# A two-layer streaming encoder on one core: norm scales moved from the weights to the activations, and the second sigmoid of stick-breaking left in its PSUM bank

## Chip, cores and metric

The kernel runs on one core of a Trainium2 chip, in one launch. The metric is the device time in microseconds (us) from start to end; less is better. TensorE multiplies, VectorE, ScalarE and GpSimd do the work around it, and all DMAs of the kernel are issued from SyncE's queue. The profile calls them PE (PEld is its weight load), DVE, ACT, POOL and SP.

## What is computed

Two layers over 2048 prompt tokens and 64 sample tokens, 1024 wide, all in float32. Every layer is one mixer:

```python
xn = rms(x, norm_g)
aq, ak, av, ag, bcq, bckv, bkr, bg, cq, ck, cv, cg, mq, mg = split_in(xn @ w_in)
...                                    # four head groups A, B, C, M of 4 heads each
y = rms(heads(y, 16), out_g) * silu(gates)
x = x + y @ w_out
```

Group A is band attention, B latent attention, M attention into 256 memory tokens. Group C is stick-breaking, without a softmax:

```python
z = einsum('bqhd,bkhd->bhqk', q, k) * Dh ** -0.5
log_1m = where(mask, log_sigmoid(-z), 0.0)
tail = cumsum(log_1m, reverse=True) - log_1m
w = where(mask, exp(log_sigmoid(z) + tail), 0.0)
```

So a weight is sigmoid(z) of its key times the product of sigmoid(-z) over all later keys.

## The kernel before

Rows of 128 tokens are tiles: 16 prompt tiles and one for the sample, in three blocks of 6, 6 and 5. Two generators make the program together. One runs the projections (`p_stream`): for each block, layer and chunk of 256 output columns, 8 steps over the 1024 inputs. The other runs attention (`attention`): units of two query tiles and four key tiles, group after group; a unit's scores, transposes and products with V are three stages that run on different units at the same time. A rule of target positions interleaves both, and the framework's scheduler then orders each engine's queue, which runs in that order.

Float32 products are made from two roundings, high and low: x = xh + xl and w = wh + wl, and a step is three matmuls (L402, L403, L405: xh wh, xh wl, xl wh; for narrow chunks the first two are one, L400).

`weights` (L297) makes both parts of a chunk. It loads blocks of two steps (`raw`, 128 x 2 x 256). For each step GpSimd multiplies by the norm's gain `gc`, a column with one value per input row, and rounds (L304); VectorE makes the low part from the same product (L305). The tiles `wh` are 8, as many as one chunk has steps, so the next chunk's first write waits until the last row tile of this chunk has used the buffer.

`prep` (L239) makes the parts of the activations. For each half of a row tile TensorE transposes four blocks into one bank (`ptx`, L259), ScalarE copies 512 columns to `xh` with rounding (L266), VectorE subtracts into `xl` (`sub_r`, L136). A sample tile is folded: its low part takes the free half of the 128 columns.

`Stick` (L1070) is group C. `step` makes the scores of one query tile against up to four key tiles in a bank `ps` (L855, L856; the pool `ps_st` has 5 banks, for transposes and `prep` too), adds a mask on the diagonal (L1090), and ScalarE writes sigmoid(-z) to `cc` and sigmoid(z) to `s`, both in SBUF (L1093, L1094). After that unit's round of other units' transposes and products, `s1b` copies the carry (L1109), scans on VectorE (L1110) with min(state x cc, cc), from the last key to the first, and multiplies on GpSimd (L1113). Then `s2` transposes `s` (L900), ScalarE casts to `ph` (L903), VectorE makes the low part (L136), and TensorE multiplies with V (L925). `cc` shares its buffers (tag `kr`) with a key tile of group B.

Of the kernel before, what the change touches and what calls it, by code (L numbers as in the profile page):

```python
# [7 lines left out]
F32 = mybir.dt.float32  # L8
# [56 lines left out]
def hybrid_step(  # L65
# [51 lines left out]

    mhalf = const.tile([128, 32], F32, name="mhalf")
    V.memset(mhalf, -0.5)

    NQ = 3
    qbuf = [const.tile([128, 2, 256], F32R, name=f"qbuf{i}") for i in range(NQ)]
# [113 lines left out]
        if left[tag] == 0:  # L236
            done.add(tag)

    def prep(load, norm, acts, t, split):  # L239

        xs = []
        for q in range(2):
            xs.append(pj.tile([128, 512], F32, tag="xin", name="xin", bufs=2))
            load(xs[q], q)
        yield 0
        xh = pj.tile([128, 8, 128], F32R, tag="xh", name="xh", bufs=MAXB)
        xl = pj.tile([128, 8, 128], F32R, tag="xl", name="xl", bufs=MAXB)
        st = None
        if norm:
            st = pj.tile([128, 4], F32, tag="xst", name="xst", bufs=MAXB + 1)  # L250
        acts[t] = (xh, xl, st)
        for q in range(2):
            x = xs[q]
            if norm:
                A.activation(out=xl[:, q * 4:q * 4 + 4].rearrange("p a b -> p (a b)"), in_=x, func=ACTF.Square,
                             accum_out=st[:, q:q + 1])
            pt = ps_st.tile([128, 4, 128], F32, name="ptx")
            for k in range(4):
                T.transpose(pt[:, k, :], x[:, k * 128:(k + 1) * 128], ident)  # L259
            ks = slice(q * 4, q * 4 + 4)  # L260
            if t == SAMP and split:
                A.copy(out=xl[:, ks], in_=pt)
                copy_r(xh[:, ks, 0:64], xl[:, ks, 0:64].bitcast(F32))
                sub_r(xh[:, ks, 64:128], pt[:, :, 64:128], xl[:, ks, 64:128])
            else:
                A.copy(out=xh[:, ks], in_=pt)  # L266
                sub_r(xl[:, ks], pt, xh[:, ks])
            yield 1024
        if norm:
            V.tensor_tensor(out=st[:, 2:3], in0=st[:, 0:1], in1=st[:, 1:2], op=ALU.add)  # L270
            V.tensor_scalar(out=st[:, 2:3], in0=st[:, 2:3], scalar1=1.0 / 1024, scalar2=EPS,
                            op0=ALU.mult, op1=ALU.add)
            rpow(st[:, 3:4], st[:, 2:3], 1)
# [22 lines left out]

    def weights(job, c0, w, out):  # L297

        gc = job.gcols()

        def split(raw, k):
            hl = pj.tile([128, 512], F32R, tag="wh", name="wh", bufs=8)
            h, lo = hl[:, 0:w], hl[:, w:2 * w]
            G.tensor_scalar(out=h, in0=raw, scalar1=gc[:, k:k + 1], scalar2=1.0, op0=ALU.mult, op1=ALU.mult)  # L304
            V.scalar_tensor_tensor(out=lo, in0=raw, scalar=gc[:, k:k + 1],  # L305
                                   in1=h.bitcast(F32), op0=ALU.mult, op1=ALU.subtract)
            out.append((hl[:, 0:2 * w], h, lo))

        n = 2
        src = job.wsrc[:, 8 * c0:8 * (c0 + w)].rearrange("p (k c) -> p k c", k=8)  # L310
        raws = []
        for k in range(0, 8, n):
# [2 lines left out]
            raws.append(raw)  # L315
            yield 0
            if k > 0:
                for i in range(n):
                    split(raws[-2][:, i, 0:w], k - n + i)
                    yield 0  # L320
        for i in range(n):
            if i:
                yield 0
            split(raws[-1][:, i, 0:w], 8 - n + i)

    def p_stream(jobs):
        chunks = [(j,) + c for j in jobs for c in j.chunks]
# [32 lines left out]
        def start_prep(j, t):  # L360

            if (j, t) not in ready:
                ready.add((j, t))
                begin(j)
                preps[j, t] = prep(j.loader(t), j.norm, j.acts, t, j.folds(t))
                next(preps[j, t])

        def prep_tile(j, t):
# [700 lines left out]

    class Stick(Unit):  # L1070
        def s1a(self):
            self.sb, self.cc, self.k = [], [], 0

        def more(self):
            return self.k < self.n
# [1 line left out]
        def step(self):  # L1077
# [11 lines left out]
            if mask is not None:  # L1089
                V.tensor_tensor(out=ps[:, w - 128:w], in0=ps[:, w - 128:w], in1=mask, op=ALU.add)  # L1090
            s = s_tile()
            cc = at.tile([128, 512], F32, tag="kr", name="cc", bufs=4)
            A.activation(out=cc[:, 0:w], in_=ps[:, 0:w], func=ACTF.Sigmoid, scale=-0.125)  # L1093
            A.activation(out=s[:, 0:w], in_=ps[:, 0:w], func=ACTF.Sigmoid, scale=0.125)  # L1094
            self.sb.append(s)
            self.cc.append(cc)
            self.k += 1

        def s1b(self):
            p = self.pair  # L1100
            carry = p.setdefault("carry", [None, None])
            for i, (a, e) in enumerate(self.ranges):
                w = (e - a) * 128
                s, cc = self.sb[i], self.cc[i]
                r = at.tile([128, 513], F32, tag="r", name="r", bufs=3)
                if carry[i] is None:
                    G.memset(r[:, w:w + 1], 1.0)
                else:
                    V.tensor_copy(r[:, w:w + 1], carry[i][:, 0:1])  # L1109
                V.tensor_tensor_scan(r[:, 0:w][:, ::-1], cc[:, 0:w][:, ::-1], cc[:, 0:w][:, ::-1], r[:, w:w + 1],  # L1110
                                     ALU.mult, ALU.min)
                carry[i] = r
                G.tensor_tensor(out=s[:, 0:w], in0=s[:, 0:w], in1=r[:, 1:w + 1], op=ALU.mult)  # L1113

    def load_kv(d, g, h, c, n, sample):
        kv = at.tile([128, 2, 512], F32R, tag="kv", name="kv", bufs=5)
# [454 lines left out]
```

## Time and profile before

| | |
|---|---|
| median of 3 runs | 3382.83 us (3377.99 to 3388.35) |
| profiled execution, time | 3392.03 us |
| profiled execution, span | 3390.2 us |
| TensorE busy | 3177.9 us (94%), 24486 matmuls |
| VectorE busy | 2728.9 us (80%) |
| ScalarE busy | 1939.0 us (57%) |
| GpSimd busy | 1598.4 us (47%) |
| granted TensorE clock, mean | 0.985 |

Busy shares are means over stages with different limits, and matmuls overlap each other, so a busy TensorE isn't one at its peak; the number of matmuls in a stretch tells more.

### The profile page before, as it was taken

What the parts mean: (1) busy time and instruction counts of PE and PEld (TensorE: products, weight loads), DVE (VectorE), ACT (ScalarE), POOL (GpSimd) and SP (SyncE); (2) the same over time, 40 slices, a digit from 0 to 9 for tenths busy, and PEclk for the clock granted to TensorE, in tenths of its full rate; (3) what the DMA queues carried; (4) which work ended last, traced back from release to release, by engine and by line L of the source; (5) the groups of instructions that cost most, each with busy time, mean ns of one, the idle gap of its engine ahead of it and who ended that gap; (6) DMA issues with size and microseconds to landing.
All of it is one profiled execution on the core that took longest, in us unless ns stands there. A gap on an engine that the chain in (4) does not pass through costs nothing. (4 is left out here: it accounts for less than half of the span.)

```text
span 3390.2 us, 75857 instructions
## 1 busy us (share of the span) xinstructions
PE 3177.9 (94%) x24486; PEld 3029.8 (89%) x24486; DVE 2728.9 (80%) x7976; ACT 1939.0 (57%) x5336; POOL 1598.4 (47%) x2353
## 2 busy tenths in 40 slices
PE   8999899899999998999999899988999999999898
PEld 7899899789999988999999788978898998888898
DVE  5686777999788789887778977899878888776994
ACT  4455655567665555566556665656646566654651
POOL 4564455666344256542434635477424454112563
PEclk9999999999999998999999999999999999999999
DMA  6555776435656656565566567634455766556534
GB/s 198 168 147 165 205 203 191 131 101 155 172 155 192 194 165 166 141 191 154 145 186 193 146 177 209 194 111 118 140 142 160 207 193 192 151 149 179 153 110 147
DMA packets 576123, 558.95 MB, mean 165 GB/s; under 512 B 70960, under 2 KB 478000, under 8 KB 575728
## 3 DMA queue, kind: packets, MB, share of 16 engines
q1 hardware_dynamic: 575728, 554.10, 58.3%
q8 instruction: 196, 3.21, 0.4%
q14 instruction: 199, 1.63, 0.2%
HBM read 378.21 MB, written 173.75 MB: 163 GB/s over the span
## 5 line engine op out<-in xcount | busy, mean ns | idle before, releaser
L403 PE MATMUL pp<-wh,xh 128*128 128x256 f32 x4416 | 1268.4, 291 | 33.6 <-DVE wh L305 32.3
L402 PE MATMUL pp<-wh,xh 128*128 128x256 f32 x4416 | 1259.8, 290 | 21.9 <-ACT ev L437 14.4
L405 PE MATMUL pp<-wh,xl 128*128 128x256 f32 (+1 forms) x4416 | 1250.5, 285 | 0.6 <-DVE xl L136 0.4
L403 PEld LDWEIGHTS pp<-wh,xh 128*128 128x128 f32 x4416 | 839.9, 191 | 64.0 <-DVE wh L305 51.3
L402 PEld LDWEIGHTS pp<-wh,xh 128*128 128x128 f32 x4416 | 837.5, 191 | 39.2 <-ACT ev L437 18.5
L405 PEld LDWEIGHTS pp<-wh,xl 128*128 128x128 f32 x4416 | 845.1, 192 | 9.3 <-DVE xl L136 0.8
L304 POOL TENSOR_SCALAR wh<-raw,gc 128x256 fp32r<-128x256 f32 (+1 forms) x848 | 500.1, 604 | 301.6 <-PE pp L405 146.3
L925 PE MATMUL ot<-ph,kv 128*128 128x256 f32 (+1 forms) x3104 | 591.8, 294 | 34.3 <-DVE ph L136 18.8
L903 ACT CAST ph<-pt 128x512 fp32r<-128x512 f32 (+2 forms) x840 | 451.0, 551 | 259.6 <-PE pt L900 231.0
L136 DVE TENSOR_TENSOR ph<-pt,ph 128x512 fp32r<-128x512 f32 (+2 forms) x840 | 525.9, 634 | 68.7 <-ACT ph L903 64.8
L900 PE MATMUL pt<-identr,s 128*128 128x128 f32 x3056 | 509.7, 277 | 25.2 <-POOL s L1113 8.0
L925 PEld LDWEIGHTS ot<-ph,kv 128*128 128x128 f32 x3104 | 458.7, 191 | 56.5 <-DVE ph L136 28.0
L1113 POOL TENSOR_TENSOR s<-s,r 128x512 f32<-128x512 f32 (+3 forms) x328 | 359.6, 1102 | 311.4 <-DVE r L1110 136.9
L305 DVE SCALAR_TENSOR_TENSOR wh<-raw,gc,wh 128x256 fp32r<-128x256 f32 (+1 forms) x848 | 472.5, 582 | 25.0 <-POOL wh L304 22.9
L1110 DVE TENSOR_TENSOR_SCAN r<-cc,r 128x512 f32<-128x512 f32 (+3 forms) x328 | 406.5, 1250 | 15.9 <-ACT cc L1093 14.4
L139 POOL TENSOR_TENSOR st<-st,mhalf 128x4 f32<-128x4 f32 (+1 forms) x312 | 283.3, 913 | 270.9 <-DVE st L463 240.4
L855 PE MATMUL ps<-kv,qbuf 128*128 128x512 f32 (+3 forms) x1024 | 376.7, 371 | 25.7 <-DVE ph L136 5.4
L900 PEld LDWEIGHTS pt<-identr,s 128*128 128x128 f32 x3056 | 361.8, 141 | 43.6 <-POOL s L1113 12.4
L856 PE MATMUL ps<-kv,qbuf 128*128 128x512 f32 (+3 forms) x1024 | 351.1, 345 | 0.0
L437 ACT ACTIVATE ev<-pp,xst 128x256 f32<-128x256 f32 (+1 forms) x424 | 199.9, 473 | 161.7 <-PE pp L405 118.4
L1093 ACT ACTIVATE cc<-ps 128x512 f32<-128x512 f32 (+3 forms) x328 | 178.2, 544 | 192.5 <-DVE ps L1090 153.7
L1051 ACT ACTIVATE s<-s,nm 128x512 f32<-128x512 f32 (+3 forms) x328 | 212.6, 651 | 107.2 <-DVE nm L1043 74.3
(171 smaller groups left out, 5128.9 us busy)
## 6 DMA issues: line engine op xcount, KB each, us to landing
raw<-in_w_in SPq DMA_DIRECT2D x288, 256.0 KB, 3.5
kv<-kvC SPq DMA_DIRECT2D x128, 256.0 KB, 4.3
kv<-kvB SPq DMA_DIRECT2D x128, 256.0 KB, 4.4
kv<-kvA SPq DMA_DIRECT2D x96, 256.0 KB, 4.5
raw<-in_w_out SPq DMA_DIRECT2D x96, 256.0 KB, 3.4
y<-y SPq DMA_DIRECT2D x136, 128.0 KB, 2.5
xin<-y SPq DMA_DIRECT2D x64, 256.0 KB, 3.5
qC<-kt SPq DMA_DIRECT2D x34, 256.0 KB, 3.0
```

The costliest lines, as they stand in the source:

```text
L136: (eng or V).tensor_tensor(out=dst, in0=src, in1=hi.bitcast(F32), op=ALU.subtract)
L304: G.tensor_scalar(out=h, in0=raw, scalar1=gc[:, k:k + 1], scalar2=1.0, op0=ALU.mult, op1=ALU.mult)
L305: V.scalar_tensor_tensor(out=lo, in0=raw, scalar=gc[:, k:k + 1], in1=h.bitcast(F32), op0=ALU.mult, op1=ALU.subtract)
L402: T.matmul(pp, lhsT=xh[:, k], rhs=wh, start=(k == 0), stop=False)
L403: T.matmul(pp, lhsT=xh[:, k], rhs=wl, start=False, stop=end)
L405: T.matmul(pp[:, 0:w], lhsT=xl[:, k], rhs=wh, start=False, stop=(k == 7))
L855: T.matmul(ps[:, 0:w], lhsT=q[:, 0, qs], rhs=kt[:, c0:c0 + w], start=True, stop=False)
L900: T.transpose(pt[:, (u + x) * 128:(u + x + 1) * 128], self.p_of(i, j), ident)
L903: A.copy(out=ph[:, 0:w], in_=pt[:, 0:w])
L925: T.matmul(ot[:, e * lo, il[0]:il[0] + n], lhsT=p["vt"](j), rhs=phl[:, e, u * 128:(u + n) * 128], start=start and e == 0, stop=stop and e ...
L1110: V.tensor_tensor_scan(r[:, 0:w][:, ::-1], cc[:, 0:w][:, ::-1], cc[:, 0:w][:, ::-1], r[:, w:w + 1], ALU.mult, ALU.min)
L1113: G.tensor_tensor(out=s[:, 0:w], in0=s[:, 0:w], in1=r[:, 1:w + 1], op=ALU.mult)
```

## The change

Two edits in one.

Norm scales: the gain is no longer multiplied into the weights but into the transposed activations. In `prep` ScalarE makes four scaled copies, one per block of 128 inputs with its column of `gc`, and VectorE makes the low part with the same column, also in four. `weights` is left with splitting: ScalarE copies two steps at once with rounding, GpSimd subtracts. VectorE has no part in it. The tiles `wh` hold two steps each, and are 4.

Stick-breaking: sigmoid(z) is made first, then sigmoid(-z) overwrites the scores in their bank, and the scan reads it there. Its second input is a column of ones, broadcast: min(state x cc, 1). Carry, scan and product move from `s1b` to the end of `step`.

```diff
+    one = const.tile([128, 1], F32, name="one")
+    V.memset(one, 1.0)
...
-    def prep(load, norm, acts, t, split):
+    def prep(load, norm, acts, t, split, gc):
...
-            if t == SAMP and split:
-                A.copy(out=xl[:, ks], in_=pt)
+            fold = t == SAMP and split
+            hi, cs = (xl, slice(64, 128)) if fold else (xh, slice(0, 128))
+            lo = xh if fold else xl
+
+            for k in range(4):
+                kk = q * 4 + k
+                A.activation(out=hi[:, kk], in_=pt[:, k], func=ACTF.Copy, scale=gc[:, kk:kk + 1])
+            for k in range(4):
+                kk = q * 4 + k
+                V.scalar_tensor_tensor(out=lo[:, kk, cs], in0=pt[:, k, cs], scalar=gc[:, kk:kk + 1],
+                                       in1=hi[:, kk, cs].bitcast(F32), op0=ALU.mult, op1=ALU.subtract)
+            if fold:
                 copy_r(xh[:, ks, 0:64], xl[:, ks, 0:64].bitcast(F32))
-                sub_r(xh[:, ks, 64:128], pt[:, :, 64:128], xl[:, ks, 64:128])
-            else:
-                A.copy(out=xh[:, ks], in_=pt)
-                sub_r(xl[:, ks], pt, xh[:, ks])
...
-        gc = job.gcols()
-
-        def split(raw, k):
-            hl = pj.tile([128, 512], F32R, tag="wh", name="wh", bufs=8)
-            h, lo = hl[:, 0:w], hl[:, w:2 * w]
-            G.tensor_scalar(out=h, in0=raw, scalar1=gc[:, k:k + 1], scalar2=1.0, op0=ALU.mult, op1=ALU.mult)
-            V.scalar_tensor_tensor(out=lo, in0=raw, scalar=gc[:, k:k + 1],
-                                   in1=h.bitcast(F32), op0=ALU.mult, op1=ALU.subtract)
-            out.append((hl[:, 0:2 * w], h, lo))
-
         n = 2
+
+        def split(raw):
+            hl = pj.tile([128, n, 512], F32R, tag="wh", name="wh", bufs=4)
+            h, lo = hl[:, :, 0:w], hl[:, :, w:2 * w]
+            A.copy(out=h, in_=raw)
+            G.tensor_tensor(out=lo, in0=raw, in1=h.bitcast(F32), op=ALU.subtract)
+            for i in range(n):
+                out.append((hl[:, i, 0:2 * w], h[:, i], lo[:, i]))
+
...
-            cc = at.tile([128, 512], F32, tag="kr", name="cc", bufs=4)
-            A.activation(out=cc[:, 0:w], in_=ps[:, 0:w], func=ACTF.Sigmoid, scale=-0.125)
             A.activation(out=s[:, 0:w], in_=ps[:, 0:w], func=ACTF.Sigmoid, scale=0.125)
+
+            cc = ps[:, 0:w]
+            A.activation(out=cc, in_=cc, func=ACTF.Sigmoid, scale=-0.125)
+            carry = p.setdefault("carry", [None, None])
+            r = at.tile([128, 513], F32, tag="r", name="r", bufs=3)
+            if carry[i] is None:
+                G.memset(r[:, w:w + 1], 1.0)
+            else:
+                V.tensor_copy(r[:, w:w + 1], carry[i][:, 0:1])
+            V.tensor_tensor_scan(r[:, 0:w][:, ::-1], cc[:, ::-1], one.to_broadcast([128, w]), r[:, w:w + 1], ALU.mult, ALU.min)
+            carry[i] = r
+            G.tensor_tensor(out=s[:, 0:w], in0=s[:, 0:w], in1=r[:, 1:w + 1], op=ALU.mult)
             self.sb.append(s)
-            self.cc.append(cc)
             self.k += 1
 
         def s1b(self):
-            p = self.pair
...
+            pass
```

The scheduler orders the queues anew. On VectorE, at the diagonal unit of tiles 10 and 11 of one head in layer 0 (the rows named `r<-cc,r` are the scan, `wh<-raw,gc,wh` the weights' low part), it stood like this before:

```order
L1090 TENSOR_TENSOR ps<-ps,tri 128x128
L947 TENSOR_TENSOR opark<-ob,opark 128x2x64
L1110 SCALAR_TENSOR_TENSOR r<-cc,r 128x384
L305 SCALAR_TENSOR_TENSOR wh<-raw,gc,wh 128x256 x2
L1110 SCALAR_TENSOR_TENSOR r<-cc,r 128x512
L305 SCALAR_TENSOR_TENSOR wh<-raw,gc,wh 128x256
L1109 COPY r<-r 128x1
```

and in the changed kernel, at the same unit of one head:

```order
L1093 TENSOR_TENSOR ps<-ps,tri 128x128
L1105 SCALAR_TENSOR_TENSOR r<-ps,r,one 128x384
L1104 COPY r<-r 128x1
L1105 SCALAR_TENSOR_TENSOR r<-ps,r,one 128x512
L1104 COPY r<-r 128x1
L138 TENSOR_TENSOR ph<-pt,ph 128x512 x2
```

The weight split is gone from between the scans, and the scan reads the bank `ps`.

On ScalarE, where the last of the three units of tiles 10 and 11 begins in one head (`ph<-pt` is the cast of transposed weights, `ev<-pp` the eviction of a projection), the order before was:

```order
L903 CAST ph<-pt 128x512
L931 COPY os<-ot 128x256
L497 CAST kt<-ptk 128x256
L903 CAST ph<-pt 128x384
L1093 ACTIVATE cc<-ps 128x512
L1094 ACTIVATE s<-ps 128x512
L437 ACTIVATE ev<-pp,xst 128x256
L1093 ACTIVATE cc<-ps 128x512
```

and in the changed kernel:

```order
L906 CAST ph<-pt 128x512
L934 COPY os<-ot 128x256
L500 CAST kt<-ptk 128x256
L906 CAST ph<-pt 128x384
L312 CAST wh<-raw 128x2x256 x3
L440 ACTIVATE ev<-pp,xst 128x256
L1095 ACTIVATE s<-ps 128x512
L1098 ACTIVATE ps<-ps 128x512
```

Three weight copies now stand ahead of the eviction and the sigmoids, and the sigmoids have changed places.

## Rows read from the trace of the kernel before

**Rows 1.** The page: busy us, share of the span and instructions of each engine.
```profile
span 3390.2 us, 75857 instructions
...
PE 3177.9 (94%) x24486; PEld 3029.8 (89%) x24486; DVE 2728.9 (80%) x7976; ACT 1939.0 (57%) x5336; POOL 1598.4 (47%) x2353
```

**Rows 2.** Busy us (instructions) by stretch: five with stick-breaking, then one without.
```profile
core 0: us, PE busy (x) PEld busy (x) DVE busy (x) ACT busy (x) POOL busy (x), PEclk, DMA share, GB/s
600.00:800.00 200.00, 180.28 (x1376) 168.42 (x1375) 188.08 (x363) 129.42 (x310) 136.47 (x164) 1.00 0.42 115
1200.00:1500.00 300.00, 279.01 (x2088) 262.69 (x2086) 265.50 (x595) 170.86 (x422) 163.43 (x214) 0.97 0.58 162
1800.00:1900.00 100.00, 94.74 (x762) 91.92 (x761) 88.25 (x262) 63.89 (x201) 56.44 (x81) 0.98 0.59 170
2200.00:2400.00 200.00, 176.50 (x1304) 163.15 (x1302) 190.13 (x351) 125.29 (x296) 143.07 (x160) 0.98 0.39 109
3100.00:3300.00 200.00, 183.79 (x1388) 172.66 (x1387) 189.93 (x352) 119.36 (x265) 116.05 (x137) 0.98 0.51 141
sum 1000.00, PE 914.31 PEld 858.84 DVE 921.88 ACT 608.81 POOL 615.45; mean PE 182.86 PEld 171.77 DVE 184.38 ACT 121.76 POOL 123.09
...
800.00:1200.00 400.00, 391.36 (x3095) 378.02 (x3095) 320.65 (x1056) 234.89 (x654) 166.13 (x267) 1.00 0.64 180
```

**Rows 3.** The same five stretches, instructions of L305, L1110 and L266 alone, sums.
```profile
sum 1000.00, DVE 135.31; mean DVE 27.06
...
sum 1000.00, DVE 352.92; mean DVE 70.58
...
sum 1000.00, ACT 26.32; mean ACT 5.26
```

**Rows 4.** Groups, busy us and mean ns: split by line, scan, product by form.
```profile
L304 POOL TENSOR_SCALAR wh<-raw,gc 128x256 fp32r<-128x256 f32 (+1 forms) x848 | 500.1, 604 | 301.6 <-PE pp L405 146.3
...
L305 DVE SCALAR_TENSOR_TENSOR wh<-raw,gc,wh 128x256 fp32r<-128x256 f32 (+1 forms) x848 | 472.5, 582 | 25.0 <-POOL wh L304 22.9
...
L1110 DVE TENSOR_TENSOR_SCAN r<-cc,r 128x512 f32<-128x512 f32 x224 | 327.1, 1470 | 6.8 <-ACT cc L1093 6.4 <-issue 0.2
L1113 POOL TENSOR_TENSOR s<-s,r 128x512 f32<-128x512 f32 x224 | 279.4, 1253 | 189.3 <-DVE r L1110 68.2 <-ACT s L1094 27.0 <-ACT ph L903 12.6
```

**Rows 5.** Groups by form: what stands nearest to the new copies and scalings.
```profile
L136 DVE TENSOR_TENSOR xl<-ptx,xh 128x512 fp32r<-128x512 f32 x136 | 92.2, 682 | 16.7 <-ACT xh L266 16.3
...
L266 ACT CAST xh<-ptx 128x512 fp32r<-128x512 f32 x136 | 79.4, 595 | 33.0 <-PE ptx L259 32.2
...
L501 DVE SCALAR_TENSOR_TENSOR kt<-ptk,qg,kt 128x256 fp32r<-128x256 f32 x102 | 48.3, 473 | 3.7 <-ACT kt L500 3.6
L255 ACT ACTIVATE xl<-xin 128x512 fp32r<-128x512 f32 x76 | 48.0, 635 | 51.7 <-DMA xin<-in_x_prompt 24.6 <-DMA xin<-x 21.0 <-DMA xin<-in_x_sample 3.7
...
L1066 DVE SCALAR_TENSOR_TENSOR opark<-opark,f,ob 128x64 f32<-128x64 f32 x192 | 45.1, 274 | 14.7 <-PE ob L941 14.4
...
L437 ACT ACTIVATE ev<-pp,xst 128x160 f32<-128x160 f32 x32 | 12.7, 396 | 3.7 <-PE pp L405 2.9 <-PE ot L925 0.6
```

**Rows 6.** VectorE: a scan in the timeline; additions 256 wide, groups by form.
```profile
651.64 1.27 DVE L1110 TENSOR_TENSOR_SCAN r<-cc,r 128x512 f32<-128x512 f32 x1
...
L474 DVE TENSOR_TENSOR nrm<-ev,st 128x256 f32<-128x256 f32 x106 | 58.2, 549 | 17.2 <-POOL st L139 10.0 <-DMA o_akp<-nrm 4.8 <-PE ptk L494 1.4
...
L838 DVE TENSOR_TENSOR xr<-pp,xr 128x256 f32<-128x256 f32 x128 | 52.7, 414 | 33.4 <-PE pp L405 17.9 <-DMA xr<-x 13.8 <-DMA xr<-in_x_prompt 1.2
```

**Rows 7.** Waits: total us, times, longest; GpSimd, then TensorE.
```profile
POOL wh L304 <- PE pp L405: 146.3, 39, 28.5
...
POOL wh L304 <- PE pp L403: 88.1, 25, 18.2
...
PE pp L403 <- DVE wh L305: 32.3, 49, 2.1
...
PE pp L402 <- ACT ev L437: 14.4, 13, 4.1
```

More of the change, by code (lines that the diff above doesn't have):

```diff
@@ L317, in weights @@
             if k > 0:
[L318 to L322, printed above, removed]
+                split(raws[-2][:, :, 0:w])
                 yield 0
-            split(raws[-1][:, i, 0:w], 8 - n + i)
+        split(raws[-1][:, :, 0:w])
     def p_stream(jobs):
@@ L364, in start_prep @@
                 begin(j)
-                preps[j, t] = prep(j.loader(t), j.norm, j.acts, t, j.folds(t))
+                preps[j, t] = prep(j.loader(t), j.norm, j.acts, t, j.folds(t), j.gcols())
                 next(preps[j, t])
@@ L1071, in s1a @@
         def s1a(self):
-            self.sb, self.cc, self.k = [], [], 0
+            self.sb, self.k = [], 0
         def more(self):
@@ L1091, in step @@
             s = s_tile()
-            cc = at.tile([128, 512], F32, tag="kr", name="cc", bufs=4)
-            A.activation(out=cc[:, 0:w], in_=ps[:, 0:w], func=ACTF.Sigmoid, scale=-0.125)
             A.activation(out=s[:, 0:w], in_=ps[:, 0:w], func=ACTF.Sigmoid, scale=0.125)
+            cc = ps[:, 0:w]
[9 more added lines that the diff above has]
+            G.tensor_tensor(out=s[:, 0:w], in0=s[:, 0:w], in1=r[:, 1:w + 1], op=ALU.mult)
             self.sb.append(s)
-            self.cc.append(cc)
             self.k += 1
         def s1b(self):
-            p = self.pair
[L1101 to L1113, printed above, removed]
+            pass
     def load_kv(d, g, h, c, n, sample):
```

## The prediction, made before the changed kernel was run

> **What bounds the kernel now.** I read the page's busy times first. TensorE is busy for 3177.9 of 3390.2 us and VectorE for 2728.9, while ScalarE has 1939.0 and GpSimd 1598.4 [rows 1]. Averages hide stages, so I then read busy time by stretch. Five stretches hold most of the scans of stick-breaking (group C). In these 1000 us VectorE is busy for 921.9 and TensorE for only 914.3, with 6918 matmuls (the five counts added). In 800 to 1200 us, which holds almost no scan, TensorE is busy for 391.4 of 400 us and does 3095 matmuls, 7.74 per us against 6.92 [rows 2]. So there are two regimes: outside the scans TensorE sets the pace; inside them VectorE is nearly full and TensorE goes without work for 86 us and runs slower. What fills VectorE there: the scans take 352.9 us and the weight split (L305) 135.3 us [rows 3]. The waits agree: the largest wait of TensorE shown is for the low half of a weight from VectorE, 32.3 us [rows 7].
>
> **Part 1, the weights.** VectorE loses all 848 operations of L305, 472.5 us, of which 135.3 us lie in the five stretches [rows 3, 4]. GpSimd loses 848 scalings (500.1 us) and gets 424 subtractions of two blocks at once. The nearest row is the product of stick-breaking, also two inputs, 512 wide: 1.253 us [rows 4]. 424 x 1.253 = 531 us, at most 31 us more; I count nothing, since GpSimd has the most slack. ScalarE gets 424 copies. The nearest row is its pass over 512 elements in SBUF, 0.635 us [rows 5]: 424 x 0.635 = 269 us. Some 29% of the split lies in the five stretches (135.3 of 472.5), so at most 122 copies, 77 us.
>
> **Part 2, the norm scales in `prep`.** 136 half tiles take one copy (0.595 us) and one subtraction (0.682 us) [rows 5]. Each becomes four scaled copies 128 wide on ScalarE, with a column as scale, and four combined operations on VectorE. The row nearest to such a copy is the eviction of 160 columns, 0.396 us; I take 0.38: 4 x 0.38 - 0.595 = +0.925 us, x 136 = +126 us on ScalarE. For VectorE I go between 0.473 us at 256 and 0.274 us at 64 columns and take 0.34: 4 x 0.34 - 0.682 = +0.68 us, x 136 = +92 us. A third of it (26.3 of 79.4 us) is in the five stretches [rows 3, 5]: +42 us on ScalarE, +30 us on VectorE there. This work runs one tile ahead of its matmuls, so it is load and not delay, except for the very first tile, where nothing covers the two halves: 2 x (0.925 + 0.68) = 3 us on the path.
>
> **Part 3, the scan from its bank.** ScalarE's work is the same two sigmoids; the second now writes the bank. VectorE's scan reads one tensor from PSUM and a single broadcast column instead of the same SBUF tile twice. No row shows such a scan. A scan of 512 takes 1.470 us on average; one that I looked up in the timeline took 1.27 us [rows 4, 6]. The additions 256 wide tell which way a PSUM input goes: 0.414 us from a bank against 0.549 us from SBUF [rows 6]. So I bound the new scan by 1.27 and 1.47 us and take the middle, 7% less: -25 us of the 352.9 us. They speak against a slower scan too. [...]
>
> **The order.** Scan, carry and product now stand right behind the sigmoids in `step`, not after the other units' transposes, so the bank's release isn't queued behind them; the printed order of VectorE shows mask, scan and carry together, with no weight split between the two scans. On ScalarE the copies stand between the casts of `ph` and the sigmoids, three in a row at one place shown.
>
> **The sum.** In the five stretches VectorE goes from 921.9 to 921.9 - 135.3 + 30 - 25 = 792 us, ScalarE from 608.8 to 608.8 + 77 + 42 = 728 us. VectorE is no longer the fullest. What comes next is TensorE itself, and the two ends of the gain are its rows [rows 2]: if only its idle share falls from 86 us to that of the stretch without scans (8.6 of 400), the same work needs 914.3 / 0.978 = 935 us, 65 us less; if it also reaches 7.74 matmuls per us, 6918 need 894 us, 106 us less. I take 75 us, near the lower end, since ScalarE at 728 of 925 us (79%) queues more than its 61% today, and it stands twice in each chain from scores to output. Below, the gain is bounded by nothing at all (the rivals). In the other 2390 us VectorE gets lighter by 337 - 62 = 275 us and ScalarE heavier by 192 + 84 = 276 us: they change places, TensorE is the bound, I count 0. Sum: 3392.0 - 75 + 3 = 3320 us against the profiled execution's own time of 3392.0 us. The runs' median, 3382.8 us, is 0.27% below that execution, so I move it by the same 72 us: **3311 us**.
>
> **Rivals.**
> *ScalarE as a gate (slower).* GpSimd waited 146.3 + 88.1 = 234 us in 64 waits, 3.7 us each, for matmuls to release a weight buffer [rows 7]. There are still as many buffers as one chunk of weights needs, so the first writer still waits, and that is now ScalarE. Behind its copies stand casts of `ph`, evictions and sigmoids that TensorE needs at once, where behind GpSimd's stood little. If half of the 234 us reaches TensorE, 117 us are lost and the gain of 72 is outweighed: 3428 us. It decides from about a third (75 of 234). For it: the three copies in a row. Against it: they stand between evictions and casts that wait for the same matmuls, and ScalarE has slack. 15%.
> *The bank is held too long (no change).* A bank of scores is now held through the scan, 1.27 to 1.47 us more, and for its turn at VectorE; five banks serve scores, transposes and `prep`. If banks decide in the stretches, some 270 scans (352.9 us at 1.3 us) x 1.4 us / 5 banks = 76 us eat the gain: 3386 us. Against it: the scan moves forward and its engine is emptier. 12%.
> *All of it (faster still).* The stretches reach 7.74 matmuls per us (-106 us) and the rest gains some 20 us of waits for VectorE; 3260 us. For it: fewer reads of two SBUF inputs leave GpSimd's operations shorter too. [...] 15%.
> My forecast has 58%.
>
> **How the numbers follow.** A change under 0.3% can't be told from none here. The forecast and the faster rival lie clear of it; of the bank rival I give half to no change, a quarter to each side. With a little of the forecast's own spread: faster 0.74, same 0.07, slower 0.19. The range runs from 3245 us, a little below the faster rival, up to 3390 us, which takes in the bank rival; the gate (15%) and some 4% below are left out.
>
> **What would show it.** Right: in the stretches with scans VectorE below 87% busy, TensorE above 96%; the scan of 512 at 1.27 to 1.47 us; the weight copy near 0.64 us and the subtraction near 1.25 us; ScalarE near 2330 us in all (1939 + 269 + 126). Wrong: ScalarE waiting for TensorE at the weight copy for over 100 us while TensorE waits for ScalarE (gate), or TensorE's scores and transposes waiting for the scan (banks). If TensorE's idle time in the stretches stays near 86 us though VectorE is lighter, the latency of the chain and not VectorE's load was the bound.

## Result and the profile after

The changed kernel takes 3330.36 us (median of 4 runs, 3327.82 to 3335.09) against 3380.41 us before (4 runs). The ratio is 0.9848, with a 95% interval of 0.9831 to 0.9866: 50 us less, where 72 were forecast (3311 us). The profiled execution took 3332.5 us, with a span of 3330.7 us. The page of after, against [rows 1]:

```profile
span 3330.7 us, 75584 instructions
...
PE 3144.7 (94%) x24486; PEld 3009.3 (90%) x24486; DVE 2481.0 (74%) x7561; ACT 2223.6 (67%) x6192; POOL 1546.7 (46%) x1929
```

VectorE lost 248 us, ScalarE gained 285. Where the time went is not in the five stretches of the prediction any more, since all stages have moved. So I take, for every kernel, the six **stick stages** (first to last scan of each round of group C, on a grid of 10 us), and call the remainder the **rest**. The busy times by stretch of before, then of after:

```profile
core 0: us, PE busy (x) PEld busy (x) DVE busy (x) ACT busy (x) POOL busy (x), PEclk, DMA share, GB/s
150.00:280.00 130.00, 125.73 (x1013) 122.19 (x1012) 105.94 (x231) 71.41 (x186) 85.61 (x128) 0.99 0.58 156
...
2200.00:2410.00 210.00, 184.53 (x1359) 170.28 (x1358) 199.65 (x372) 129.10 (x303) 149.70 (x169) 0.98 0.41 115
...
sum 1060.00, PE 960.89 PEld 901.98 DVE 977.68 ACT 642.38 POOL 684.54; mean PE 160.15 PEld 150.33 DVE 162.95 ACT 107.06 POOL 114.09
```

```profile
160.00:280.00 120.00, 118.53 (x983) 116.40 (x982) 85.60 (x186) 79.26 (x201) 76.68 (x105) 1.00 0.58 160
...
2170.00:2360.00 190.00, 178.25 (x1382) 168.93 (x1381) 167.61 (x332) 139.90 (x325) 124.42 (x148) 1.00 0.45 125
...
sum 990.00, PE 943.00 PEld 901.15 DVE 838.68 ACT 726.12 POOL 604.89; mean PE 157.17 PEld 150.19 DVE 139.78 ACT 121.02 POOL 100.81
```

The row to compare is that of the fifth stage: 1382 matmuls in 190 us now, 1359 in 210 us before. Over all six, before did 7247 matmuls in 1060 us (6.837 per us), after 7397 in 990 us (7.472). At the old pace 7397 take 1082 us, so the stick stages gave **92 us**. The rest does 17117 matmuls at 7.313 per us instead of 7.410; at the old pace they take 2310 us, now 2341: it **took back 31 us**. The forecast had 75 and 0 (and 3 for the first tile). Some of the 92 us may be TensorE's clock: both traces show two granted levels, 1.0 and 0.5 of full speed, and the stick stages spend 44 us at 0.5 in before, 14 us in after. By half the difference, an estimate from these figures, that is 15 us; no run tells whether it is a cause or follows from shorter waits.

The groups of after that answer to [rows 4, 5]:

```profile
L1105 DVE TENSOR_TENSOR_SCAN r<-ps,r,one 128x512 f32<-128x512 f32 x224 | 283.3, 1274 | 31.1 <-ACT ps L1098 30.4
L1107 POOL TENSOR_TENSOR s<-s,r 128x512 f32<-128x512 f32 x224 | 248.8, 1112 | 175.3 <-DVE r L1105 144.4 <-DVE mst L1348 8.2 <-DVE xst L278 6.1
L313 POOL TENSOR_TENSOR wh<-raw,wh 128x512 fp32r<-128x512 f32 x400 | 517.3, 1313 | 303.5 <-ACT wh L312 291.4 <-DMA raw<-in_w_mem 4.8 <-issue 3.6
...
L312 ACT CAST wh<-raw 128x512 fp32r<-128x512 f32 (+1 forms) x424 | 249.6, 628 | 50.6 <-PE pp L406 25.5 <-PE pp L408 13.2 <-issue 4.4
L269 ACT ACTIVATE xh<-ptx,gc 128x128 fp32r<-128x128 f32 x544 | 156.6, 400 | 26.5 <-PE ptx L261 21.7 <-PE pp L406 4.2
L272 DVE SCALAR_TENSOR_TENSOR xl<-ptx,gc,xh 128x128 fp32r<-128x128 f32 x544 | 152.7, 342 | 33.0 <-ACT xh L269 31.8 <-DMA raw<-in_w_in 0.7
```

The scan of 512 fell from 1470 to 1274 ns and the product on GpSimd from 1253 to 1112 ns. The new pieces cost about what was forecast: 628 ns for the weight copy (635), 1313 for the subtraction (1253), 400 and 342 ns for the four pieces of `prep` (380 and 340). The waits of after, TensorE and ScalarE (us in total, times, longest):

```profile
PE ps L858 <- DVE r L1105: 13.6, 22, 1.5
...
PE pp L406 <- POOL wh L313: 7.1, 10, 1.6
...
ACT wh L312 <- PE pp L406: 25.5, 5, 12.2
ACT wh L312 <- PE pp L408: 13.2, 27, 0.9
```

The wait for a weight's low half fell from 32.3 us [rows 7] to 7.1. ScalarE stands 39 us at the weight buffers, where GpSimd stood 234; the bank is waited for 13.6 us. Neither of the two rivals that would have cost time decided.

### The profile page after: what moved, and what is told of

It reads as the page before. It is cut to its first block, busy times and chain, and to the rows that moved or that the text cites. A ratio compares the mean times of both kernels' runs of the same rounds, so it can differ in the third digit from the quotient of the medians.

```text
span 3330.7 us, 75584 instructions
## 1 busy us (share of the span) xinstructions
PE 3144.7 (94%) x24486; PEld 3009.3 (90%) x24486; DVE 2481.0 (74%) x7561; ACT 2223.6 (67%) x6192; POOL 1546.7 (46%) x1929
## 4 chain that ended last, share of the span: by engine, by line
PE 37%; DMA 9%; DVE 9%; ACT 3%; issue 3%; POOL 2%; SPq 1%; POOLq 0%; DVEq 0%; ACTq 0%
PE pp L405 6%; PE pp L406 6%; PE pp L408 6%; PE ot L928 5%; PE pt L903 5%; PE ps L858 3%; PE ps L859 2%; DVE r L1105 2%; DMA y<-y 1%; PE ps L861 1%; DVE ph L138 1%; DMA xin<-x 1%; PE ob L944 1%; DMA qr<-qr 1%; PE ptx L261 1%
## 5 line engine op out<-in xcount | busy, mean ns | idle before, releaser
L405 PE MATMUL pp<-wh,xh 128*128 128x256 f32 x4416 | 1262.5, 290 | 18.6 <-ACT ev L440 6.7
L313 POOL TENSOR_TENSOR wh<-raw,wh 128x512 fp32r<-128x512 f32 (+1 forms) x424 | 538.3, 1289 | 320.5 <-ACT wh L312 308.2
L928 PE MATMUL ot<-ph,kv 128*128 128x256 f32 (+1 forms) x3104 | 583.3, 293 | 28.5 <-DVE ph L138 13.9
L138 DVE TENSOR_TENSOR ph<-pt,ph 128x512 fp32r<-128x512 f32 (+2 forms) x840 | 525.5, 634 | 88.2 <-ACT ph L906 83.3
L1107 POOL TENSOR_TENSOR s<-s,r 128x512 f32<-128x512 f32 (+3 forms) x328 | 316.8, 968 | 303.4 <-DVE r L1105 261.6
L858 PE MATMUL ps<-kv,qbuf 128*128 128x512 f32 (+3 forms) x1024 | 375.9, 370 | 32.5 <-DVE r L1105 13.6
L141 POOL TENSOR_TENSOR st<-st,mhalf 128x4 f32<-128x4 f32 (+1 forms) x312 | 270.1, 872 | 281.1 <-DVE st L466 244.1
L1105 DVE TENSOR_TENSOR_SCAN r<-ps,r,one 128x512 f32<-128x512 f32 (+3 forms) x328 | 360.0, 1106 | 52.7 <-ACT ps L1098 50.3
L312 ACT CAST wh<-raw 128x512 fp32r<-128x512 f32 (+1 forms) x424 | 249.6, 628 | 50.6 <-PE pp L406 25.5
L1002 ACT ACTIVATE s<-s,nm 128x256 f32<-128x256 f32 (+4 forms) x272 | 169.6, 626 | 130.3 <-DVE nm L991 83.5
```

Source lines behind the costliest of these rows:

```text
L138: (eng or V).tensor_tensor(out=dst, in0=src, in1=hi.bitcast(F32), op=ALU.subtract)
L313: G.tensor_tensor(out=lo, in0=raw, in1=h.bitcast(F32), op=ALU.subtract)
L405: T.matmul(pp, lhsT=xh[:, k], rhs=wh, start=(k == 0), stop=False)
L858: T.matmul(ps[:, 0:w], lhsT=q[:, 0, qs], rhs=kt[:, c0:c0 + w], start=True, stop=False)
L928: T.matmul(ot[:, e * lo, il[0]:il[0] + n], lhsT=p["vt"](j), rhs=phl[:, e, u * 128:(u + n) * 128], start=start and e == 0, stop=stop and e ...
L1105: V.tensor_tensor_scan(r[:, 0:w][:, ::-1], cc[:, ::-1], one.to_broadcast([128, w]), r[:, w:w + 1], ALU.mult, ALU.min)
```

## The experiments

The two theories at the start: **load** (VectorE was full in the stick stages, and taking the weight split off it is the main gain, as the prediction had it) and **lock** (VectorE instructions on SBUF and GpSimd hold each other up, and the scan, for which GpSimd's product and then the transposes wait, no longer does). Matmuls per us were read as above. The ratio, with its 95% interval, is to the runs of before in the same round, whose medians went from 3380.4 to 3384.1 us; the stages are cut on a grid of 10 us, so small differences in the last two columns say little.

| run | time, us | ratio to before | stick stages | rest |
|---|---|---|---|---|
| before | 3380.4 | 1 | 6.837 | 7.410 |
| after | 3330.4 | 0.9848 [0.9831, 0.9866] | 7.472 | 7.313 |
| e1_norm | 3402.5 | 1.0053 [1.0035, 1.0070] | 6.990 | 7.307 |
| e2_stick | 3331.3 | 0.9848 [0.9825, 0.9871] | 7.301 | 7.376 |
| e3_cc_sbuf | 3388.2 | 1.0020 [1.0007, 1.0033] | 7.066 | 7.331 |
| e4_prep | 3409.0 | 1.0076 [1.0053, 1.0099] | 7.257 | 7.170 |
| e5_mix | 3338.7 | 0.9873 [0.9858, 0.9887] | 7.454 | 7.291 |
| e9_prep4 | 3347.8 | 0.9900 [0.9885, 0.9914] | 7.163 | 7.387 |
| e10_nogain | 3319.7 | 0.9816 [0.9801, 0.9831] | 7.432 | 7.375 |
| e7_pool_v | 3294.4 | 0.9746 [0.9730, 0.9763] | 7.473 | 7.442 |
| e6_lo_v | 3311.8 | 0.9792 [0.9774, 0.9810] | 7.359 | 7.443 |
| e13_act_load | 3313.0 | 0.9799 [0.9779, 0.9818] | 7.395 | 7.394 |
| e11_pv_prep | 3371.4 | 0.9973 [0.9961, 0.9986] | 7.307 | 7.267 |
| e14_pool_load | 3346.2 | 0.9890 [0.9866, 0.9913] | 7.328 | 7.356 |

**One edit alone.** `e1_norm` is the change with the old class `Stick`; `e2_stick` is the old kernel with the new one. The core of each, against the change:

```diff
-            V.tensor_tensor_scan(r[:, 0:w][:, ::-1], cc[:, ::-1], one.to_broadcast([128, w]), r[:, w:w + 1], ALU.mult, ALU.min)
+                V.tensor_tensor_scan(r[:, 0:w][:, ::-1], cc[:, 0:w][:, ::-1], cc[:, 0:w][:, ::-1], r[:, w:w + 1],
+                                     ALU.mult, ALU.min)
```

```diff
-            A.copy(out=h, in_=raw)
-            G.tensor_tensor(out=lo, in0=raw, in1=h.bitcast(F32), op=ALU.subtract)
+            G.tensor_scalar(out=h, in0=raw, scalar1=gc[:, k:k + 1], scalar2=1.0, op0=ALU.mult, op1=ALU.mult)
+            V.scalar_tensor_tensor(out=lo, in0=raw, scalar=gc[:, k:k + 1],
+                                   in1=h.bitcast(F32), op0=ALU.mult, op1=ALU.subtract)
```

> The norm edit alone (weights split by ScalarE and GpSimd, gains in prep); group C as before, with the scan from SBUF in s1b. If VectorE's load in the stick stages was the bound, most of the gain is here, since of the 137 us that VectorE lost in those stages 105 net are the weights': ratio to before 0.987 to 0.993 (3337 to 3358 us), with the stick stages at over 7.2 matmuls per us and the rest of the program slower than before by some 30 us. If the order of the scan and its PSUM bank were the lever, this kernel gains nothing or loses the 30 us of the rest: 1.000 to 1.010.

> The stick edit alone (sigmoid(-z) in its bank, scan in step); weights and prep as before. By VectorE's load it saves only the 46 us of shorter scans: ratio 0.990 to 0.997, VectorE still at 90% or more in the stick stages. If the order and the bank were the lever: 0.983 or less. If banks held too long bind: PE waits for the scan at scores and transposes of over 30 us and a ratio over 1.000.

The norm edit alone, which takes VectorE's 472 us of weight splits away, is slower by 0.5%. The stick edit alone is the whole gain, with VectorE still at 90.5% in the stick stages; its ratio, 0.9848, is close to the 0.983 that was expected of order and bank. So load is not the main gain. It is not nothing either: in the stick stages the norm edit raises the pace from 6.837 to 6.990 alone and from 7.301 to 7.472 on top of the stick edit, worth 24 and 23 us there, and the rest loses 33 and 20 us. Alone it also stretches the scan from SBUF, from 1470 to 1573 ns, so `e1_norm` mixes load and lock.

**What of the stick edit it is.** `e3_cc_sbuf` keeps the new order and the broadcast column, and puts sigmoid(-z) back into SBUF:

```diff
-            cc = ps[:, 0:w]
-            A.activation(out=cc, in_=cc, func=ACTF.Sigmoid, scale=-0.125)
+            cc = at.tile([128, 512], F32, tag="kr", name="cc", bufs=4)[:, 0:w]
+            A.activation(out=cc, in_=ps[:, 0:w], func=ACTF.Sigmoid, scale=-0.125)
```

> The changed kernel with sigmoid(-z) written to SBUF again; order, broadcast ones and norm edit stay. If the PSUM source is what made the scan shorter, the scan of 512 goes back to 1.40 to 1.47 us, and the kernel is 0.2 to 0.6% slower than the changed one (3337 to 3350 us). If it was the second read of a whole SBUF tile that cost, the scan stays at 1.27 us and the time with it. If the bank, held through the scan, was costing, this one is faster than the changed kernel: below 3325 us, with PE's wait for the scan at the scores (13.6 us) gone.

The gain is gone, and more than was expected: 58 us slower than the change, where 7 to 20 were expected. Against `e1_norm` it is 14 us faster, which is what the new order and the column of ones give by themselves there. The scan and the product, group by form, in this run:

```profile
L1105 DVE TENSOR_TENSOR_SCAN r<-cc,r,one 128x512 f32<-128x512 f32 x224 | 342.2, 1538 | 15.5 <-ACT cc L1098 13.7 <-POOL r L1102 1.1
L1107 POOL TENSOR_TENSOR s<-s,r 128x512 f32<-128x512 f32 x224 | 284.4, 1276 | 168.0 <-DVE r L1105 143.7 <-DVE mst L1347 6.5 <-DVE mst L1348 4.1
```

It could still be the recurrence that runs faster from PSUM. `e5_mix` starts from this kernel and gives the scan the raw scores in the bank as its second input:

```diff
-            V.tensor_tensor_scan(r[:, 0:w][:, ::-1], cc[:, ::-1], one.to_broadcast([128, w]), r[:, w:w + 1], ALU.mult, ALU.min)
+            V.tensor_tensor_scan(r[:, 0:w][:, ::-1], cc[:, ::-1], ps[:, 0:w][:, ::-1], r[:, w:w + 1], ALU.mult, ALU.max)
```

> The changed kernel with sigmoid(-z) in SBUF as the scan's first input, as in the run with it back in SBUF, but with the raw scores in the PSUM bank as its second input and a maximum in place of the minimum; so the weights of group C are other numbers, and the bank is held through the scan as in the changed kernel. Theory of the two SBUF inputs (VectorE and GpSimd hinder each other whenever both inputs of a VectorE operation lie in SBUF): one input in PSUM is enough, so the scan of 512 takes 1.26 to 1.32 us, the product on GpSimd 1.10 to 1.16 us, and the time is 3325 to 3350 us. Rival (the recurrence itself is faster with its first input in PSUM, whatever the second is): the scan stays at 1.45 to 1.57 us and the time at 3370 us or more.

```profile
L1103 DVE TENSOR_TENSOR_SCAN r<-cc,r,ps 128x512 f32<-128x512 f32 x224 | 282.6, 1271 | 28.5 <-ACT cc L1096 27.2
L1105 POOL TENSOR_TENSOR s<-s,r 128x512 f32<-128x512 f32 x224 | 248.1, 1110 | 177.8 <-DVE r L1103 144.9 <-DVE mst L1346 8.6 <-DVE mst L1345 5.2
```

Here the weights of group C are other numbers, but the work has the same form. 1271 ns and 3338.7 us: one input out of SBUF is enough, whichever it is. Durations (minimum, median, maximum, all widths) say the same. Before, then after:

```profile
L1110 DVE TENSOR_TENSOR_SCAN r<-cc,r x328: 453/1271/2183, 156.2 to 3299.1; 128x512 f32<-128x512 f32 x100, 128x128 f32<-128x128 f32 x28, 128x384 f32<-128x384 f32 x28, 128x256 f32<-128x256 f32 x8
```

```profile
L1105 DVE TENSOR_TENSOR_SCAN r<-ps,r,one x328: 445/1270/1285, 161.6 to 3240.0; 128x512 f32<-128x512 f32 x100, 128x128 f32<-128x128 f32 x28, 128x384 f32<-128x384 f32 x28, 128x256 f32<-128x256 f32 x8
```

The median is unchanged; only the tail, up to 2183 ns, is gone. The scan never was slower in SBUF: it stood and waited while GpSimd worked. One place in the timeline of before, VectorE and then GpSimd:

```profile
3265.09 1.28 DVE L1110 TENSOR_TENSOR_SCAN r<-cc,r 128x512 f32<-128x512 f32 x1
3266.47 0.15 DVE L1109 COPY r<-r 128x1 f32<-128x1 f32 x1
3266.54 2.17 DVE L1110 TENSOR_TENSOR_SCAN r<-cc,r 128x512 f32<-128x512 f32 x1
...
3266.53 1.09 POOL L1113 TENSOR_TENSOR s<-s,r 128x512 f32<-128x512 f32 x1 [1.35 <-DVE r L1110]
```

The first scan releases its product on GpSimd, the product begins just ahead of the second scan, and the second scan ends 1.08 us after the product does. In the trace of before 91 of the 224 scans of 512 take over 1300 ns. All 91 end 1.07 to 1.09 us after a GpSimd instruction that was running when they began (twice it started up to 44 ns later), in 59 cases this product. So stick-breaking mostly held itself up. With one input in PSUM no scan waits so: in after the longest of the 328 takes 1285 ns. Nor does the PSUM source cost the scan more in itself: a median of 1270 ns against 1271.

**What the norm edit costs.** Its parts are `prep` in four pieces, copies on ScalarE and subtractions on GpSimd. `e9_prep4` is `e2_stick` with the four pieces of the change and a column of ones; `e10_nogain` is the change with the old `prep`, and so leaves the gains out. One half of each edit, the copy on ScalarE:

```diff
-                A.copy(out=xh[:, ks], in_=pt)
+                A.activation(out=hi[:, kk], in_=pt[:, k], func=ACTF.Copy, scale=one[:, 0:1])
```

```diff
-                A.activation(out=hi[:, kk], in_=pt[:, k], func=ACTF.Copy, scale=gc[:, kk:kk + 1])
+                A.copy(out=xh[:, ks], in_=pt)
```

> The stick-breaking edit alone (3331.3 us when it ran), with prep cut into four scaled copies on ScalarE and four combined operations on VectorE as in the changed kernel, but with a column of ones as the scale; the weights are split and scaled as before the change. Theory that the four pieces in prep cost what the norm edit loses outside the scan stages: 3350 to 3375 us, with about 7.31 matmuls per us outside the stick stages where the stick edit alone had 7.38. Rival, that the weight copies on ScalarE cost it: 3326 to 3340 us.

> The changed kernel with prep as it was before the change, so that the norm gains of the projections are left out of the result altogether: the weights are split by ScalarE and GpSimd, nothing multiplies by the gains. Theory that the four pieces in prep eat what the weight split gives: 3285 to 3312 us. Rival, that the weight split by ScalarE and GpSimd is worth nothing because VectorE's load was not what held TensorE: 3322 to 3338 us, that is the time of the changed kernel.

Both came out between the theories. The four pieces cost 16.5 us (3331.3 to 3347.8), all in the stick stages there; put back into the change, they cost 10.6 us (3319.7 to 3330.4), there in the rest. The new weight split is worth 11.5 us (3331.3 to 3319.7), with the pace of the stick stages up from 7.301 to 7.432. So on top of the stick edit the norm edit adds up to about nothing.

`e4_prep` and `e11_pv_prep` replace the four pieces by three passes of 512, in which the input tile holds the product. In `e4_prep` GpSimd subtracts, in `e11_pv_prep` VectorE (and there the weights are split as in `e7_pool_v`):

```diff
+            tmp = x.rearrange("p (k c) -> p k c", k=4)
+            V.tensor_tensor(out=tmp, in0=pt, in1=gc[:, ks].unsqueeze(2).to_broadcast([128, 4, 128]), op=ALU.mult)
+            A.copy(out=hi[:, ks], in_=tmp)
+            G.tensor_tensor(out=lo[:, ks, cs], in0=tmp[:, :, cs], in1=hi[:, ks, cs].bitcast(F32), op=ALU.subtract)
```

> The changed kernel with another prep: VectorE multiplies the whole bank by the gains once (into the xin tile), ScalarE rounds 512 columns once, GpSimd subtracts. ScalarE loses about 130 us, VectorE about 90 us, GpSimd gains about 170 us. If the 30 us lost outside the stick stages come from the four-piece prep, they come back: 3295 to 3318 us. If they come from the weight copies on ScalarE, the time stays within 10 us of the changed kernel. If the xin tile, held longer, delays the next load, slower than 3340 us.

> The faster variant (weights split by GpSimd and VectorE) with prep in three passes over 512 elements: VectorE multiplies the transposed half tile by the gains into the input tile, ScalarE rounds it once, VectorE subtracts. ScalarE loses 136 times about 1 us, VectorE's share stays near 1.4 us for each half tile. Theory that the four pieces cost through ScalarE's queue: 3275 to 3290 us. Rival, that the input tile held longer or the longer chain in prep weighs more, as with GpSimd's subtraction in prep (3409.0 us): 3300 us or more.

Both are worse, though `e11_pv_prep` has less work on ScalarE than the change. Its TensorE waits:

```profile
PE ptx L261 <- DMA xin<-in_x_prompt: 22.7, 18, 6.4
PE ptx L261 <- DMA xin<-y: 16.9, 15, 3.7
...
PE ptx L261 <- DMA xin<-x: 12.6, 11, 2.3
```

The input tile is now held until the last pass, and TensorE waits 52 us for the next load, where the kernel it is compared with, `e7_pool_v`, shows 9.2 + 6.5 us. In `e4_prep` the same three waits are 52 us against 19 in the change. That is less than half of the 77 and 79 us lost; the other part isn't broken down.

**Who should split the weights.** `e7_pool_v` takes both steps off the engines that the change gave them to, `e6_lo_v` (only the second line) one:

```diff
-            A.copy(out=h, in_=raw)
-            G.tensor_tensor(out=lo, in0=raw, in1=h.bitcast(F32), op=ALU.subtract)
+            copy_r(h, raw)
+            V.tensor_tensor(out=lo, in0=raw, in1=h.bitcast(F32), op=ALU.subtract)
```

> The changed kernel with the weight split moved off ScalarE: the high half is copied by GpSimd and the low half subtracted by VectorE, two steps at a time, both from SBUF. ScalarE loses some 424 x 0.636 = 270 us, VectorE gains 424 subtractions of 512 from two SBUF inputs. Theory that ScalarE's copies hurt outside the stick stages: the matmuls per us there rise from 7.31 to 7.37 or more, and the time stays within 10 us of the changed kernel's 3330 us. Rival, that the VectorE work and its two SBUF inputs weigh more: the scan of 512 rises above 1.30 us where it overlaps, and the time is 3345 to 3375 us.

> The changed kernel with only the low half of the weights moved, from GpSimd to VectorE; ScalarE keeps its 424 copies. It parts the two things that the faster variant with GpSimd and VectorE took away, ScalarE's copies and GpSimd's subtractions of 1.29 us. Theory that ScalarE's copies cost the changed kernel its time outside the stick stages: 3318 to 3340 us, no better than the changed kernel, and about 7.31 matmuls per us there. Rival, that GpSimd's long subtraction (the last step before a weight can be used) cost it: 3285 to 3302 us, and 7.42 or more there.

`e7_pool_v` beats both kernels and is faster than either of its theories, 2.5% under before, with VectorE busier by 138 us than in the change and the scan still at 1272 ns:

```profile
PE 3141.6 (96%) x24486; PEld 3001.0 (91%) x24486; DVE 2619.5 (80%) x7985; ACT 2021.6 (61%) x5768; POOL 1357.9 (41%) x1929
...
L313 DVE TENSOR_TENSOR wh<-raw,wh 128x512 fp32r<-128x512 f32 (+1 forms) x424 | 328.0, 784 | 20.9 <-POOL wh L135 19.0
L135 POOL TENSOR_SCALAR wh<-raw 128x512 fp32r<-128x512 f32 (+1 forms) x424 | 299.6, 718 | 290.8 <-PE pp L408 134.4
```

`e6_lo_v` lies halfway, between its two theories. Taking the subtraction off GpSimd gives 18.6 us (3330.4 to 3311.8), and the rest returns to 7.443 at once; taking the copies off ScalarE gives another 17.4 us, in the stick stages (7.359 to 7.473). The change itself had 7.472 there, with the copies on ScalarE and VectorE at 84.7% instead of 90.0%. So the copies seem to hurt where VectorE is laden too; no run parts the two. Is that ScalarE's load, or the path of a weight? `e13_act_load` adds to `e7_pool_v` two ScalarE copies into a tile that nobody reads, `e14_pool_load` two GpSimd subtractions (`two` is the identity twice, 256 columns):

```diff
             copy_r(h, raw)
+            A.copy(out=spare, in_=ident)
+            A.copy(out=spare, in_=ident)
```

```diff
             copy_r(h, raw)
+            G.tensor_tensor(out=spare, in0=two, in1=two, op=ALU.subtract)
+            G.tensor_tensor(out=spare, in0=two, in1=two, op=ALU.subtract)
...
-        trig = pj.tile([128, 64], F32, tag="trig", name="trig", bufs=4)
+        trig = pj.tile([128, 64], F32, tag="trig", name="trig", bufs=3)
```

> The faster variant (weights split by GpSimd and VectorE, 3294.4 us) with two copies of 128 columns on ScalarE beside each of the 424 splits, into a tile that nobody reads: load for ScalarE, about 0.6 us each time, 250 us in all, that no other engine waits for except through ScalarE's own queue. Theory that ScalarE's load alone cost the changed kernel its 36 us: 3315 to 3335 us, and the matmuls per us outside the stick stages fall from 7.44 to between 7.30 and 7.36. Rival, that it was the weights' own path (copy, then 1.29 us on GpSimd): 3292 to 3303 us.

> The faster variant (weights split by GpSimd and VectorE, 3294.4 us) with two subtractions of 256 columns on GpSimd beside each of the 424 splits, two inputs from SBUF, into a tile that nobody reads: 1.3 to 1.5 us each time for GpSimd, as long as the changed kernel's subtraction of a weight's low half, but on no weight's path (one of four small rope buffers is given up to make room). Theory that GpSimd's work with two SBUF inputs holds up VectorE's SBUF work wherever it runs: VectorE's 96 subtractions f of two columns rise from 0.19 us to 0.25 us or more, as in every run so far in which GpSimd subtracted the low halves, the matmuls per us outside the stick stages fall from 7.44 to 7.30 to 7.38, and the time is 3312 to 3345 us. Rival, that the subtraction cost time as the last step on a weight's path: f stays at 0.17 to 0.20 us and the time at 3290 to 3303 us.

In `e13_act_load` the copies are busy for 256 us and the time grows by 18.6 us, a little short of the range of its theory, with the rest at 7.394 where 7.36 or less was expected, but about what ScalarE's weight copies cost (17.4 us):

```profile
L315 ACT CAST spare<-identr 128x128 bf16<-128x128 f32 x424 | 128.3, 302 | 6.0
L314 ACT CAST spare<-identr 128x128 bf16<-128x128 f32 x424 | 127.9, 302 | 7.1 <-DVE identr L102 0.9
```

In `e14_pool_load` 561 us of GpSimd work that no weight depends on cost 52 us (3346.2, just above the expected 3345). So a long subtraction costs time also where it isn't the last step of a weight. But it stands in GpSimd's queue, ahead of the next weight copies and of stick-breaking's products, and one buffer of `trig` is gone too: lock and queue are not parted here. The expectation for f (0.25 us or more) failed: it rose to 0.217 only.

**The lock, seen directly.** Line 1049 subtracts two columns (f, in the softmax). Its groups (busy us, mean ns) before, after, in `e6_lo_v` and in `e14_pool_load`:

```profile
L1046 DVE TENSOR_TENSOR f<-nm 128x2 f32<-128x2 f32 x96 | 15.9, 166 | 1.4
```

```profile
L1049 DVE TENSOR_TENSOR f<-nm 128x2 f32<-128x2 f32 x96 | 30.7, 320 | 1.8
```

```profile
L1049 DVE TENSOR_TENSOR f<-nm 128x2 f32<-128x2 f32 x96 | 16.5, 172 | 1.3
```

```profile
L1053 DVE TENSOR_TENSOR f<-nm 128x2 f32<-128x2 f32 x96 | 20.8, 217 | 1.3
```

In all six kernels in which GpSimd subtracts the low halves (after, `e1_norm`, `e3_cc_sbuf`, `e4_prep`, `e5_mix`, `e10_nogain`) the mean is 252 to 337 ns; in the eight other kernels it is 166 to 217 ns. The longest f tells why. In after, `e6_lo_v` and `e14_pool_load` (minimum, median, maximum in ns):

```profile
L1049 DVE TENSOR_TENSOR f<-nm x96: 143/160/1264, 302.1 to 2978.9; 128x2 f32<-128x2 f32 x96
```

```profile
L1049 DVE TENSOR_TENSOR f<-nm x96: 143/156/728, 295.0 to 2947.6; 128x2 f32<-128x2 f32 x96
```

```profile
L1053 DVE TENSOR_TENSOR f<-nm x96: 142/160/746, 303.4 to 2983.2; 128x2 f32<-128x2 f32 x96
```

In the traces of before and after every f over 250 ns ends 6 to 20 ns after a GpSimd instruction that was running when it began. In after these are 17, and 16 of them stand behind the subtraction of a weight (mean 1313 ns), the longest too; the other, of 695 ns, stands behind `y<-y,gt`, a product of 256 columns that every kernel has. In before they are 4: the longest, of 721 ns, stands behind another product of 256 columns (`nrm<-nrm,gr`), and two, of 285 and 329 ns, behind a scaling and a copy with one input (474 and 407 ns). The longest in `e6_lo_v` and in `e14_pool_load` (728 and 746 ns) are about as long as in before, though `e14_pool_load` adds subtractions of 660 ns. One place in the timeline of after, VectorE and then GpSimd:

```profile
1006.63 0.71 DVE L477 TENSOR_TENSOR nrm<-ev,st 128x256 f32<-128x256 f32 x1
1007.26 1.23 DVE L1046 SCALAR_TENSOR_TENSOR nm<-mx,nm 128x2 f32<-128x2 f32 x1
1008.53 1.23 DVE L1049 TENSOR_TENSOR f<-nm 128x2 f32<-128x2 f32 x1
1009.68 0.68 DVE L138 TENSOR_TENSOR ph<-pt,ph 128x512 fp32r<-128x512 f32 x1
...
1005.77 5.22 POOL L313 TENSOR_TENSOR wh<-raw,wh 128x512 fp32r<-128x512 f32 x4
```

Four subtractions stand end to end for 5.22 us. Two VectorE operations on two columns, both inputs in SBUF, take 1.23 us each meanwhile, where the median is 0.16; ScalarE's exponentials wait 0.75 us for the first and 0.27 us for the second. L138, which has an input in PSUM, takes 0.68 us beside the same subtractions, as much as its mean at this width over the kernel (683 ns).

## Why the prediction was right, and where not

The time lies inside the range, on the side forecast. But the main reason given was not the main reason, and that 50 us lie so near to 72 is in part luck: the stick stages gave more than was forecast, the rest took back what was counted as nothing.

**The sum (VectorE's load).** This is the step that failed. It turned 135.3 us of VectorE's work in the five stretches [rows 3] into 65 to 106 us of time. The runs give the weight split 11.5 us (`e10_nogain` against `e2_stick`), and the whole norm edit some 23 us in the stick stages, which it loses again elsewhere. VectorE's busy share was read as the bound. But `e2_stick` runs its stick stages 7% faster with VectorE at 90.5% instead of 92.2%, and `e7_pool_v` is as fast there with 89.7% (7.473 matmuls per us) as the change with 84.7% (7.472), though it has less work on ScalarE and GpSimd.

**Part 3.** The last rival named one side of the mechanism, GpSimd's: its product did get shorter, from 1253 to 1112 ns. The scan's side was mis-sized. The middle of 1.27 and 1.47 us was taken; 1.274 was measured, the lower end: 224 x 196 ns = 44 us over the kernel, where 25 us were counted in the stretches. And the edit was priced as VectorE's time alone, when GpSimd's product and the transposes wait for the scan: in the old kernel the edit, its order included, is worth 50 us, from 3381.6 to 3331.3. The 1.27 us of [rows 6] was the median, and the mean of 1470 ns was drawn up by a tail; the row with the maximum would have shown it.

**Part 1.** The prices held: 249.6 us for the copies (269 forecast), 538.3 us for the subtractions (531). "I count nothing" for GpSimd did not: beside a subtraction of 1.3 us with two SBUF inputs VectorE's SBUF work waits (f of two columns for up to 1264 ns, where the median is 160), and moving the subtraction back to VectorE gives 18.6 us though GpSimd had the most slack.

**The rest, counted 0.** It lost 31 us. Two runs undo that: without the subtraction on GpSimd (`e6_lo_v`, same copies on ScalarE) the rest runs at 7.443 instead of 7.313, 41 us; with the old `prep` (`e10_nogain`) at 7.375, 20 us. So the subtraction is the larger part and the four pieces the smaller, and they don't simply add. How much of the first is the lock and how much GpSimd's own queue stays open: in `e14_pool_load` f rose by only 25 ns against `e7_pool_v`, and the time by 52 us.

**Part 2.** Its durations held (400 and 342 ns for 380 and 340). Its price in time did not: 10.6 to 16.5 us instead of 3.

**ScalarE.** 2223.6 us instead of some 2330: the four scaled copies overlap, 544 of 400 ns are busy for 156.6 us in all, 288 ns each. That makes 49 of the 106 us, the weight copies 19; the rest isn't broken down. ScalarE's load is not free: 256 us more cost 18.6 us.

**Rivals.** The gate needed 75 us at the weight buffers; ScalarE stood there for 39 us, and taking its copies away gave 17.4 us (`e6_lo_v` to `e7_pool_v`). The bank was to eat 76 us; TensorE's scores wait 13.6 us for it, and `e3_cc_sbuf`, which doesn't hold it through the scan, is slower. What was to be seen: VectorE at 84.7% in the stick stages (below 87, right), the scan at 1.274 (right), TensorE at 95.3% (above 96, just wrong). The sign that was to tell load from latency could not: TensorE's idle time in the stick stages fell from 99 to 47 us, but to 52 us with the stick edit alone, where VectorE was hardly lighter.

## What to carry to other kernels

Before taking a busy engine for the bound, read minimum, median and maximum of its costliest operation: here the tail far above the median was waiting that the profile shows as work, 44 us in one group of VectorE's 2729 us, and it stood where other engines wait. Keep one input of a long VectorE operation in PSUM where GpSimd works beside it (the scan of 512 took 1274 ns so, 1470 and 1538 ns in the kernels with both in SBUF), and give GpSimd short instructions rather than long two-input subtractions (f took 320 ns on average in the change, with subtractions of 1313 ns, and 192 ns in `e7_pool_v`, with copies of 718 ns): here the better division (copy of 0.72 us on GpSimd, subtraction on VectorE) took 3294 us, 36 us less than the change. A move of work to an engine with slack is to be priced at what it blocks, not at zero.

## What was not expected of the hardware

A VectorE subtraction of two columns can take 1.26 us instead of 0.16 beside GpSimd's subtraction of 512 columns, and a scan of 512 up to 2183 ns instead of 1271. One-input operations wait as well: the scaling `nm` of two columns on VectorE, before and after, went from 164 to 278 ns on average, and its longest from 368 to 1280 ns; 27 of the 144 in after are over 250 ns, and 22 of these end 22 to 30 ns after the subtraction of a weight on GpSimd:

```profile
L988 DVE TENSOR_SCALAR nm<-mx 128x2 f32<-128x2 f32 x144 | 23.7, 164 | 0.8
```

```profile
L991 DVE TENSOR_SCALAR nm<-mx 128x2 f32<-128x2 f32 x144 | 40.0, 278 | 1.3
```
